# A first head pair's attention output recombined in chunks of 128, spread over the second pair's attention

## The chip, the cores and the metric

The kernel runs on one core of a Trainium2 chip. The metric is the device time of one execution in microseconds (us); lower is better. Three executions of the kernel before gave 1064.78, 1065.20 and 1062.72 us, with a median of 1064.78 us. On-chip data lies in 128 partitions, and five engines work side by side, each through its own queue in strict order: TensorE (PE: matmuls, and transposes done as matmuls), VectorE (DVE), ScalarE (ACT), GpSimd (POOL), and SyncE (SP), whose queue issues every DMA of this kernel. An instruction that waits holds up everything behind it in its engine's queue.

## The reference

One layer of a hybrid decoder: four token mixers share an input projection, each result is gated by SiLU, and an output projection, a norm and the residual follow. The part that matters here is mixer A, attention with four heads of 64 channels over 2048 positions:

```python
def _dilated_mixture(q, k, v):
    outs, lses = [], []
    for window, dil in ((128, 1), (512, 4), (2048, 16)):
        o, lse = _dilated_branch(q, k, v, window, dil, slopes)
        outs.append(o); lses.append(lse)
    w = jax.nn.softmax(jnp.stack(lses), axis=0)
    return jnp.einsum('gbhs,gbhsd->bhsd', w, jnp.stack(outs))
...
y = jnp.concatenate([ya * silu(ag), yb * silu(bg), yc * silu(cg), yd * silu(dg)], -1)
y = jnp.einsum('bse,ed->bsd', y, w_out)
return x + _rms_norm(y, post_g)
```

Every head thus has three branch outputs (dilation 4, 16 and 1, in the kernel's order), which are weighted per position by three factors, added, and multiplied by the gate.

## The kernel before

**Stages.** The first stage (to about 684 us in the profile) makes all projections and mixers B, C and D. The second runs attention for two pairs of heads, and fills TensorE's free time with the part of the output projection that needs only mixers B, C and D (`partial`, for nine of the sixteen token tiles, results to memory `part_d`). The third (`final`) finishes the output projection, the norm and the residual.

**Attention.** `attention(p)` handles the heads 2p and 2p+1, one after the other. For each head it loads q and k (`q2`, `k2a`, `k2b`) and, for each of three branches, the values (`att_v`); the tiles rotate through a ring of seven. `branch` computes scores on TensorE (`ps_s`), adds the bias and takes the row minimum on VectorE (`att_p`, line 639), exponentiates on ScalarE (line 641), transposes on TensorE (`ps_pt`), splits into a high and a low part on ScalarE and VectorE (`pt_hi` line 648, `pt_lo` line 649), multiplies with the values (`ps_o`), and adds two halves of the result into the output `att_o` (ScalarE line 663, VectorE line 664). The tile `att_p` has `B_PR` = 6 buffers. A pair has three output tiles of 128 x 2048 numbers: two in one tile `o01`, and `o2` for dilation 1. `o01` of the first pair lies in the pool `big`, that of the second in the pool `po`; `o2` of both pairs lies in `po`, under one tag with one buffer.

**Weights of the branches.** After the third branch of a head, `weigh` computes the three factors and writes them to memory (`f_d`, shown as `fd`).

**Combine.** `combine` goes over the positions in chunks. For a chunk it loads the factors of both heads, each broadcast over 64 partitions (`fb`, lines 763), and the gate (`sga`, line 765); multiplies and adds on GpSimd (lines 766, 767) and VectorE (768, 769, 770, 772); splits the result on ScalarE and GpSimd (`ysa`, lines 776, 777), and stores it (`ya`, line 779). For the first pair the chunk is 256 positions (eight chunks), `fb`, `sga` and `ysa` have two buffers each, so the load of chunk i+2 needs chunk i's buffers.

**Order.** A scheduler orders each engine's queue by its own estimate of durations, with earlier written code preferred; `tc.issue_after(mark)` holds a block back until the scheduler has placed the marked instruction. `marks` lists the attention's value matmuls; the `partial` calls are spread over them. The first pair's `combine` is written ahead of the second pair's attention.

Of the kernel before, what the change touches and what calls it, by code (L numbers as in the profile page):

```python
# [9 lines left out]
F32 = mybir.dt.float32  # L10
# [8 lines left out]
P = 128  # L19
SEQ = 2048  # L20
# [16 lines left out]
MASKED = 1e30  # L37
PB = {"part": 1, "fin": 8}
N_S, N_T, N_O = 2, 3, 2
CORD = (2, 3, 0, 1)  # L40
CB0, B_PR, B_PT = 2, 6, 3


def mix_constants():
# [41 lines left out]
def hymba(ctx: ExitStack, tc: tile.TileContext, x, pre_g, w_in, sgu_g, sgu_w, sgu_b, pool_w,  # L86
# [4 lines left out]
    def r32(ap):  # L91
        return ap.bitcast(F32)
# [450 lines left out]
    def out_weights(i, eng):  # L543

        w = big.tile([P, 2, 2, DM], F32R, tag="big", name=f"wo{i}")
        for e in range(2):
            raw = p3.tile([P, DM], F32, tag="z", bufs=2, name="wo_raw")
            D.dma_start(raw, wo_src[:, i * 2 + e])
            A.activation(w[:, e, 0], raw, AF.Copy)
            eng.tensor_tensor(w[:, e, 1], raw, r32(w[:, e, 0]), ALU.subtract)  # L550
            wo[i * 2 + e] = (w[:, e, 0], w[:, e, 1])

    marks = []

    def attention(p, tab):
        o01 = (big if p == 0 else po).tile([P, 2, SEQ], F32, tag="big" if p == 0 else "o01", name="att_o01")
        o = [o01[:, 0], o01[:, 1], po.tile([P, SEQ], F32, tag="o2", name="att_o2")]
        for s in range(2):
            h = 2 * p + s
            rows = slice(s * HD, (s + 1) * HD)  # L560
# [191 lines left out]
        V.tensor_tensor(ew, ew, nm.unsqueeze(1).broadcast_to([P, 3, 16]), ALU.mult)  # L752
        D.dma_start(f_d[h].rearrange("b (q f) -> q b f", f=16), ew)

    def combine(p, o, pool, bufs, keep, step, order):

        kept = {}
        nb = step // P
        for c0 in order:
            cs = slice(c0, c0 + step)  # L760
            fb = pool.tile([P, 3, step], F32, tag="fb", bufs=bufs, name="fb")
            for s in range(2):
                D.dma_start(fb[s * HD:(s + 1) * HD], f_d[2 * p + s][:, cs].partition_broadcast(HD))
            sg = pool.tile([P, step], F32, tag="sga", bufs=bufs, name="sga")
            D.dma_start(sg, ag_d[p][:, cs])
            G.tensor_tensor(fb[:, 1], fb[:, 1], o[1][:, cs], ALU.mult)
            G.tensor_tensor(fb[:, 2], fb[:, 2], o[2][:, cs], ALU.mult)
            V.tensor_tensor(fb[:, 0], fb[:, 0], o[0][:, cs], ALU.mult)
            V.tensor_tensor(fb[:, 0], fb[:, 0], fb[:, 1], ALU.add)
            V.tensor_tensor(fb[:, 0], fb[:, 0], fb[:, 2], ALU.add)  # L770
            y = fb[:, 1]
            V.tensor_tensor(y.rearrange("p (n i r) -> p n r i", n=nb, r=16),
                            fb[:, 0].rearrange("p (n r i) -> p n r i", n=nb, r=16),
                            sg.rearrange("p (n r i) -> p n r i", n=nb, r=16), ALU.mult)
            ys = pool.tile([P, 2, step], F32R, tag="ysa", bufs=4 if keep else CB0, name="ysa")
            A.activation(ys[:, 0], y, AF.Copy)
            (V if keep else G).tensor_tensor(ys[:, 1], y, r32(ys[:, 0]), ALU.subtract)
            if not keep:
                D.dma_start(ya_d[c0 // GRP][:, :, c0 % GRP:c0 % GRP + step], r32(ys))
            kept[c0 // step] = ys  # L780
        return kept

    def load_y(t, pool):
# [29 lines left out]
    def partial(t):  # L813
        z = p3.tile([P, DM], F32, tag="z", bufs=2, name="z")
        ys = split_y(load_y(t, p3), p3, G)
        for n in range(2):
            A.activation(z[:, n * GRP:(n + 1) * GRP], out_proj(ys, range(2, 8), n, ps2, "part"), AF.Copy)
        D.dma_start(part_d[t * P:(t + 1) * P], z)
# [34 lines left out]
    po = ctx.enter_context(tc.tile_pool(name="po", bufs=1, side="right", reuse_waits="tile"))  # L853
    with ExitStack() as c2:
        pm = c2.enter_context(tc.tile_pool(name="pm", bufs=1, reuse_waits="tile"))
        p2 = c2.enter_context(tc.tile_pool(name="p2", bufs=1, reuse_waits="tile"))
        ps2 = c2.enter_context(tc.tile_pool(name="ps2", bufs=2, space=PSUM, reuse_waits="tile"))
        tab = pm.tile([P, T_HEAD], F32, name="tab")
        D.dma_start(tab, catt)
        o = attention(0, tab)  # L860
        for i in (1, 2, 3):
            out_weights(i, V if i == 2 else G)
        combine(0, o, p2, 2, False, 256, range(0, SEQ, 256))
        o = attention(1, tab)
        for t in range(npart):
            with tc.issue_after(marks[int(len(marks) * (t + spread[0]) / npart * spread[1])]):
                partial(t)
        out_weights(0, G)
# [5 lines left out]
    post_b = p4.tile([P, DM], F32, name="post_b")  # L874
    ya = [[p4.tile([P, 2, GRP], F32R, tag="ya0", bufs=4, name="ya0") for g in range(NG)]]
    ya.append(combine(1, o, p4, 2, True, GRP, [c * GRP for c in CORD]))
    for g in CORD:
        D.dma_start(r32(ya[0][g]), ya_d[g])
    D.dma_start(post_b, post_g[0].partition_broadcast(P))
    order = full[:3]  # L880
# [33 lines left out]
```

## Time and profile before

| | before |
|---|---|
| median of three executions | 1064.78 us |
| the profiled execution's own time | 1066.84 us |
| its span, first to last instruction | 1065.1 us |
| TensorE matmuls busy | 993.5 us (93%) |
| VectorE busy | 540.4 us (51%) |
| ScalarE busy | 379.6 us (36%) |
| GpSimd busy | 190.9 us (18%) |
| mean granted TensorE clock | 0.973 |
| bytes moved by DMA | 135.27 MB |

Times in the profile count from the first instruction. "Idle before, releaser" says how long an engine had been idle before an instruction and what it then waited for. A table by stretches gives, for each stretch of time, the busy microseconds of each engine, the clock that TensorE was granted (1.00 is full speed) and the share of time for which the 16 DMA engines were busy. SPq rows are DMA issues; the time in such a row is that of the issue, not of the transfer.

### The profile page before, as it was taken

The numbers are of one execution on the slowest core, as the hardware profiler recorded it, in microseconds if no ns is written. First come the engines' busy times: TensorE is split into PE (matmuls) and PEld (weight loads), VectorE is DVE, ScalarE is ACT, GpSimd is POOL, SyncE is SP. The second block draws the span as 40 slices with busy tenths as digits, with TensorE's granted clock in tenths as the row PEclk, the third lists the DMA queues.
The fourth block names the chain that finished last, engine by engine and source line by source line (L and its number), as shares of the span: only waits on it lengthen the run. The fifth ranks groups of instructions, "written<-read, shape, count | busy, mean of one in ns | idle before, by whom it ended". The sixth has DMA issues, their size and how long they took to land. (4 is left out here: it accounts for less than half of the span.)

```text
span 1065.1 us, 15690 instructions
## 1 busy us (share of the span) xinstructions
PE 993.5 (93%) x5916; PEld 855.0 (80%) x5916; DVE 540.4 (51%) x1547; ACT 379.6 (36%) x851; POOL 190.9 (18%) x195
## 2 busy tenths in 40 slices
PE   5899999999999999999999999979998779988993
PEld 5888898988877988989898787778988569867872
DVE  7611216696332422023763321287776677547898
ACT  6320222131222421122211121498877448513231
POOL 2310012211232000002210134031122351142000
PEclk9999999999999999999999999998999879989997
DMA  8530313233223331042211830395659953484776
GB/s 279 147 99 20 100 60 114 85 120 92 86 79 99 99 100 39 25 135 80 80 41 50 210 119 20 116 213 162 147 168 201 207 152 85 109 270 129 268 259 217
DMA packets 119962, 135.27 MB, mean 127 GB/s; under 512 B 14928, under 2 KB 95952, under 8 KB 117840
## 3 DMA queue, kind: packets, MB, share of 16 engines
q1 hardware_dynamic: 119888, 134.29, 43.6%
q8 instruction: 46, 0.75, 0.3%
q14 instruction: 28, 0.23, 0.1%
HBM read 97.80 MB, written 36.47 MB: 126 GB/s over the span
## 5 line engine op out<-in xcount | busy, mean ns | idle before, releaser
L95 PE MATMUL ps_t<-hh,w 128*128 128x512 f32 x1152 | 370.1, 398 | 2.3 <-DVE b_t L370 2.3
L95 PEld LDWEIGHTS ps_t<-hh,w 128*128 128x128 f32 x1152 | 216.7, 189 | 52.4 <-issue 3.4
L95 PE MATMUL ps_t<-hl,w 128*128 128x512 f32 x576 | 227.6, 395 | 0.0
L95 PE MATMUL ps_m<-w,hh 128*128 128x256 f32 x1024 | 183.8, 282 | 2.0 <-ACT hh L230 1.6
L95 PE MATMUL ps_out<-wo,yt 128*128 128x512 f32 x576 | 155.6, 414 | 6.1 <-DVE yt L798 3.1
L95 PEld LDWEIGHTS ps_m<-w,hh 128*128 128x128 f32 x1024 | 157.5, 190 | 3.9 <-ACT hh L230 2.8
L95 PE MATMUL ps_m<-w,hl 128*128 128x256 f32 x512 | 145.4, 284 | 0.2 <-DVE hl L231 0.2
L95 PEld LDWEIGHTS ps_out<-wo,yt 128*128 128x128 f32 x576 | 109.8, 198 | 31.1 <-DVE yt L798 4.4
L95 PEld LDWEIGHTS ps_t<-hl,w 128*128 128x128 f32 x576 | 108.7, 189 | 24.3 <-issue 1.4
L250 DVE TENSOR_TENSOR w<-raw,w 128x1024 fp32r<-128x1024 f32 x42 | 59.0, 1412 | 109.6 <-ACT w L248 109.4
L95 PEld LDWEIGHTS ps_m<-w,hl 128*128 128x128 f32 x512 | 97.6, 191 | 0.8 <-DVE hl L231 0.4
L641 ACT ACTIVATE att_p<-att_p,att_st 128x128 f32<-128x128 f32 (+1 forms) x192 | 86.4, 453 | 20.5 <-DVE att_st L639 20.0
L248 ACT ACTIVATE w<-raw 128x1024 fp32r<-128x1024 f32 (+1 forms) x56 | 55.0, 997 | 70.1 <-PE ps_t L95 37.6
L639 DVE CUSTOM_DVE_ANT_0 att_p<-ps_s,tab 128x128 f32<-128x128 f32 (+1 forms) x192 | 60.3, 357 | 34.5 <-PE ps_s L95 31.0
L95 PE MATMUL ps_o<-pt_hi,att_v 128*128 128x128 f32 (+1 forms) x204 | 54.4, 287 | 6.2 <-DVE att_o L664 4.2
L649 DVE TENSOR_TENSOR pt_lo<-ps_pt,pt_hi 128x512 fp32r<-128x512 f32 x80 | 51.2, 650 | 12.5 <-ACT pt_hi L648 12.1
L95 PE MATMUL ps_o<-pt_lo,att_v 128*128 128x128 f32 (+1 forms) x204 | 52.8, 294 | 3.5 <-DVE pt_lo L649 3.4
L98 PE MATMUL ps_pt<-ident,att_p 128*128 128x128 f32 x300 | 51.2, 283 | 0.8 <-ACT att_p L641 0.8
L95 PEld LDWEIGHTS ps_o<-pt_hi,att_v 128*128 128x128 f32 x204 | 40.8, 200 | 9.5 <-DVE att_o L664 4.6
L648 ACT ACTIVATE pt_hi<-ps_pt 128x512 fp32r<-128x512 f32 x80 | 44.1, 563 | 11.2 <-PE ps_pt L98 5.7
L95 PE MATMUL ps_s<-k2a,q2b 128*128 128x128 f32 (+1 forms) x128 | 37.5, 325 | 8.6 <-DMA k2a<-qk 4.4
L95 PEld LDWEIGHTS ps_o<-pt_lo,att_v 128*128 128x128 f32 x204 | 40.6, 199 | 5.9 <-DVE pt_lo L649 4.8
(160 smaller groups left out, 1319.8 us busy)
## 6 DMA issues: line engine op xcount, KB each, us to landing
raw<-in_w_in_dram SPq DMA_DIRECT2D x52, 512.0 KB
qk<-qk_s SPq DMA_DIRECT2D x16, 512.0 KB
att_v<-vd SPq DMA_DIRECT2D x8, 1024.0 KB
xr<-in_x_dram SPq DMA_DIRECT2D x16, 512.0 KB
out_dram<-z SPq DMA_DIRECT2D x15, 512.0 KB
xt<-in_x_dram SPq DMA_DIRECT2D x7, 1024.0 KB
yraw<-yb SPq DMA_DIRECT2D x16, 384.0 KB
partd<-z SPq DMA_DIRECT2D x9, 512.0 KB
```

Of the source, the lines that this page charges most:

```text
L95: return T.matmul(o, lhsT, rhs, start=start, stop=stop, skip_group_check=True)
L98: T.transpose(o, i, ident[:n, :n])
L248: A.activation(hi, raw[:, :, cs], AF.Copy, scale=sc)
L250: eng.tensor_tensor(lo, raw[:, :, cs], r32(hi), ALU.subtract)
L639: V.tensor_tensor_reduce(out=pr[:, u, :w], in0=ps[:, u, :w], in1=bb, scale=-SLOPES[h] * HD ** -0.5, scalar=3e38, op0=ALU.add, op1=ALU.min, ...
L641: A.activation(pr[:, u, :w], pr[:, u, :w], AF.Exp, bias=neg, scale=-1.0, accum_out=st[:, 1, n:n + 1])
L648: A.activation(hi, pt[:, :w], AF.Copy)
L649: V.tensor_tensor(lo, pt[:, :w], r32(hi), ALU.subtract)
```

## The change

Four edits belong together. The first pair's `o2` moves from the pool `po` into the pool `p2`, so that the two pairs no longer share memory for it. `B_PR` goes from 6 to 5, and the chunk from 256 to 128 positions, which frees the memory for it. `combine` is divided into a load and a piece of work per chunk; for the first pair the load of chunk i+1 is written ahead of the work of chunk i, and both are held back to a mark: sixteen marks spread evenly over the first 75% of the second pair's value matmuls (`PACE`). The call moves behind the second pair's attention. The second pair's own `combine` computes as before. All line numbers behind the constants shift by one, those of `combine` by up to seven, those behind it by sixteen and more.

```diff
+PACE = 0.75
-CB0, B_PR, B_PT = 2, 6, 3
+CB0, B_PR, B_PT = 2, 5, 3
...
-        o = [o01[:, 0], o01[:, 1], po.tile([P, SEQ], F32, tag="o2", name="att_o2")]
+        o = [o01[:, 0], o01[:, 1], (po if p else p2).tile([P, SEQ], F32, tag="o2", name="att_o2")]
...
-    def combine(p, o, pool, bufs, keep, step, order):
+    def combine(p, o, pool, bufs, keep, step, order, after=None):
         kept = {}
         nb = step // P
-        for c0 in order:
+        todo = list(order)
+        def load(c0):
             cs = slice(c0, c0 + step)
             fb = pool.tile([P, 3, step], F32, tag="fb", bufs=bufs, name="fb")
             for s in range(2):
                 D.dma_start(fb[s * HD:(s + 1) * HD], f_d[2 * p + s][:, cs].partition_broadcast(HD))
             sg = pool.tile([P, step], F32, tag="sga", bufs=bufs, name="sga")
             D.dma_start(sg, ag_d[p][:, cs])
+            return fb, sg
+
+        def work(c0, fb, sg):
+            cs = slice(c0, c0 + step)
             G.tensor_tensor(fb[:, 1], fb[:, 1], o[1][:, cs], ALU.mult)
...
             kept[c0 // step] = ys
+
+        if after is None:
+            for c0 in todo:
+                work(c0, *load(c0))
+            return kept
+        ahead = load(todo[0])
+        for i, c0 in enumerate(todo):
+            with after(i):
+                now, ahead = ahead, load(todo[i + 1]) if i + 1 < len(todo) else None
+                work(c0, *now)
         return kept
...
-        combine(0, o, p2, 2, False, 256, range(0, SEQ, 256))
+        o0, n0 = o, len(marks)
         o = attention(1, tab)
+        pace = (len(marks) - n0) * PACE / (SEQ // P)
+        combine(0, o0, p2, 2, False, P, range(0, SEQ, P), lambda i: tc.issue_after(marks[int(n0 + (i + 0.5) * pace)]))
```

On SP's queue, where every load is issued, the place is the beginning of the second head of the second pair: its keys (`k2b`) stand among the combine's transfers. `sga` is a gate load, `fb` a load of one head's factors, `ya` a store of a finished chunk, `std` and `partd` are other stores. Before:

```order
L765 DMA sga<-agd_71 128x256 x2
L779 DMA ya_73<-ysa 256x1x256
L763 DMA fb<-fd_86 64x3x256
L779 DMA ya_73<-ysa 256x1x256
L763 DMA fb<-fd_87 64x3x256
L763 DMA fb<-fd_86 64x3x256
L763 DMA fb<-fd_87 64x3x256
L735 DMA std_84<-sT 16x16x8 x2
L818 DMA partd<-z 128x1024
L569 DMA k2b<-qk_69 64x2048 x2
```

Now:

```order
L785 DMA ya_73<-ysa 256x1x128
L765 DMA fb<-fd_86 64x3x128
L765 DMA fb<-fd_87 64x3x128
L785 DMA ya_73<-ysa 256x1x128
L765 DMA fb<-fd_86 64x3x128
L765 DMA fb<-fd_87 64x3x128
L736 DMA std_84<-sT 16x16x8 x2
L767 DMA sga<-agd_71 128x128
L570 DMA k2b<-qk_69 64x2048 x2
L767 DMA sga<-agd_71 128x128
```

The transfers are half as wide, and the gate load of the fifth chunk, which needs the third chunk's buffer, now stands ahead of the keys. In both orders the factors of a chunk follow the store of the chunk two before it.

On VectorE the place is between the third and the fifth chunk before (the first row is the third chunk's last product, the last row the fifth chunk's first):

```order
L772 TENSOR_TENSOR fb<-fb,sga 128x2x16x8
L649 TENSOR_TENSOR pt_lo<-ps_pt,pt_hi 128x512
L770 TENSOR_TENSOR fb<-fb 128x256
...
L772 TENSOR_TENSOR fb<-fb,sga 128x2x16x8
L649 TENSOR_TENSOR pt_lo<-ps_pt,pt_hi 128x512 x2
L639 ISA att_p,att_st<-ps_s,tab 128x256
L639 ISA att_st 128x1
L639 ISA att_p,att_st<-ps_s,tab 128x256
L639 ISA att_st 128x1
L768 TENSOR_TENSOR fb<-fb,att_o_5880 128x256
```

and now between the thirteenth and the fifteenth chunk, where the first and the last row have the same meaning:

```order
L778 TENSOR_TENSOR fb<-fb,sga 128x16x8
L774 TENSOR_TENSOR fb<-fb,att_o_5880 128x128
...
L775 TENSOR_TENSOR fb<-fb 128x128
L665 TENSOR_TENSOR att_o_7131<-ps_o,att_o_7131 64x4x16x8
L640 ISA att_p,att_st<-ps_s,tab 128x256
L640 ISA att_st 128x1
L640 ISA att_p,att_st<-ps_s,tab 128x256
L640 ISA att_st 128x1
L776 TENSOR_TENSOR fb<-fb 128x128
L778 TENSOR_TENSOR fb<-fb,sga 128x16x8
L650 TENSOR_TENSOR pt_lo<-ps_pt,pt_hi 128x512
L774 TENSOR_TENSOR fb<-fb,att_o_5880 128x128
```

The dots stand for two `att_p` rows of 256 in each list, in the second with one `pt_lo` row of 512. A chunk's products are now mixed with attention rows up to the end of the second pair, where they stood together in its first half before.

## The prediction

> **What bounds the kernel now.** I read the head of the page first, then a table by stretches of the attention and final stages.
>
> ```profile
> PE 993.5 (93%) x5916; PEld 855.0 (80%) x5916; DVE 540.4 (51%) x1547; ACT 379.6 (36%) x851; POOL 190.9 (18%) x195
> ```
>
> TensorE is busy for 93% of the span, so time is won only where it idles or runs at a low clock.
>
> ```profile
> core 0: us, PE busy (x) PEld busy (x) DVE busy (x) ACT busy (x) POOL busy (x), PEclk, DMA share, GB/s
> 684.00:800.00 116.00, 105.32 (x737) 96.11 (x738) 87.72 (x327) 100.44 (x308) 22.94 (x22) 0.96 0.69 178
> 800.00:880.00 80.00, 64.71 (x354) 54.67 (x353) 54.04 (x166) 42.24 (x136) 30.83 (x37) 0.85 0.81 187
> 880.00:920.00 40.00, 40.00 (x289) 37.21 (x289) 29.24 (x99) 33.26 (x101) 4.56 (x6) 0.99 0.25 59
> 920.00:960.00 40.00, 33.82 (x136) 26.17 (x136) 17.49 (x23) 8.05 (x15) 12.91 (x8) 0.91 0.79 242
> ```
>
> The stretch 800 to 880 us is the one with the combine of the first pair. TensorE idles 80.00 - 64.71 = 15.3 us there, and its clock is 0.85; of the 64.71 busy us, 0.15 x 64.71 = 9.7 us are due to the clock. Right behind, with the combine over, it idles not at all. So 25.0 us is what the stretch can give. What it waits for is in the list of waits of that stretch:
>
> ```profile
> DVE fb L768 <- DMA fb<-fd: 17.6, 5, 5.0
> ...
> ACT att_o L663 <- POOL fb L767: 5.9, 1, 5.9
> ...
> PE ps_st L98 <- DVE pt_lo L649: 3.7, 1, 3.7
> PE ps_s L95 <- DVE att_st L639: 3.4, 2, 3.2
> PE ps_o L95 <- DVE att_o L664: 3.3, 3, 2.4
> PE ps_o L95 <- DVE pt_lo L649: 2.9, 2, 2.7
> ```
>
> TensorE waits for VectorE's attention rows, and VectorE has been standing before a combine row whose factors had not landed: five times, 17.6 us. The second row is the shared memory: ScalarE's first write into the second pair's `o2` waits 5.9 us for GpSimd's last read of the first pair's. In order of time:
>
> ```profile
> 869.78 0.90 POOL L767 TENSOR_TENSOR fb<-fb,att_o 128x256 f32<-128x256 f32 x1
> ...
> 870.72 1.08 ACT L663 ACTIVATE att_o<-ps_o 64x512 f32<-64x512 f32 x2 [5.87 <-POOL fb L767]
> ...
> 872.85 0.33 PE L95 MATMUL ps_o<-pt_hi,att_v 128*128 128x128 f32 x1 [2.38 <-DVE att_o L664]
> ...
> 875.12 0.44 PE L95 MATMUL ps_o<-pt_hi,att_v 128*128 128x128 f32 x1 [0.54 <-DVE att_o L664]
> ```
>
> Thus 2.4 + 0.5 us of TensorE's idle time are due to `o2`; with the clock after it (0.84 on 16.50 busy us, 2.6 us) this is 5.5 us:
>
> ```profile
> 800.00:820.00 20.00, 17.27 (x116) 15.63 (x114) 13.32 (x56) 13.33 (x51) 5.80 (x8) 0.91 0.89 183
> ...
> 860.00:880.00 20.00, 16.50 (x75) 13.47 (x74) 13.58 (x31) 7.36 (x20) 8.60 (x10) 0.84 0.59 136
> ```
>
> The other 19.5 us belong to the 17.6 us of waits for factors: 1.1 us lost for each us VectorE waits.
>
> **The change part by part.** *Memory of its own for `o2`.* It takes away 5.5 us, whole: the reads of the first pair's `o2` then hold up nothing.
>
> *The first wait stays.* The first chunk needs the second head's factors, which exist only when that head's weights are stored.
>
> ```profile
> 804.96 1.26 SPq L763 DMA_DIRECT2D fb<-fd  x2
> ...
> 810.00 0.42 DVE L768 TENSOR_TENSOR fb<-fb,att_o 128x256 f32<-128x256 f32 x1 [4.85 <-DMA fb<-fd]
> ...
> 811.08 0.39 PE L95 MATMUL ps_o<-pt_lo,att_v 128*128 128x256 f32 x1 [2.73 <-DVE pt_lo L649]
> ...
> L639 DVE CUSTOM_DVE_ANT_0 att_p<-ps_s,tab 128x128 f32<-128x128 f32 x38 | 9.0, 281 | 1.7 <-PE ps_s L95 1.7
> ```
>
> The two loads are issued at 804.96, and VectorE stands until 810.00. In the new order the first two chunks' rows stand four narrow `att_p` rows earlier (4 x 0.281 = 1.1 us, the last row). I keep the 2.7 us gap, the clock (0.09 x 17.27 = 1.6 us) and add that with a small copy, 1.3 us: 5.6 us. Bounds: 3 (half the bytes land sooner) to 7.
>
> *The waits behind it* decide. A chunk's load follows the store of the chunk two before, in both orders. So VectorE's wait is the turnaround (last product, split, store issued, factors issued, landed) less the attention work that stands between. Before:
>
> ```profile
> 835.53 0.59 DVE L772 TENSOR_TENSOR fb<-fb,sga 128x256 f32<-128x256 f32 x1
> ...
> 837.58 0.60 DVE L772 TENSOR_TENSOR fb<-fb,sga 128x256 f32<-128x256 f32 x1
> ...
> 840.23 0.55 SPq L779 DMA_DIRECT2D ya<-ysa  x1
> 840.83 1.28 SPq L763 DMA_DIRECT2D fb<-fd  x2
> ...
> 846.21 0.43 DVE L768 TENSOR_TENSOR fb<-fb,att_o 128x256 f32<-128x256 f32 x1 [4.97 <-DMA fb<-fd]
> ...
> 850.95 0.43 DVE L768 TENSOR_TENSOR fb<-fb,att_o 128x256 f32<-128x256 f32 x1 [1.12 <-DMA fb<-fd]
> ```
>
> The fourth chunk's product ends at 838.18, the sixth's factors have landed at 850.95: 12.8 us. The third's ends at 836.12, the fifth starts at 846.21: 10.1 us, of which VectorE worked 5.1 and stood 4.97. For the work between I use the mean rows:
>
> ```profile
> L649 DVE TENSOR_TENSOR pt_lo<-ps_pt,pt_hi 128x512 fp32r<-128x512 f32 x28 | 18.9, 683 | 5.4 <-ACT pt_hi L648 5.3
> L639 DVE CUSTOM_DVE_ANT_0 att_p<-ps_s,tab 128x256 f32<-128x256 f32 x42 | 16.2, 415 | 6.2 <-PE ps_s L95 4.1 <-PE ps_pt L98 2.0
> L664 DVE TENSOR_TENSOR att_o<-ps_o,att_o 64x512 f32<-64x512 f32 x21 | 14.4, 685 | 1.9 <-ACT att_o L663 1.5
> ```
>
> In the new order, from the thirteenth chunk's product to the fifteenth's first row, stand four `att_p` (1.66), two `pt_lo` (1.37), one `att_o` (0.69) and about 1.5 us of combine rows: 5.2 us. VectorE is 29.24/40 = 73% busy in an undisturbed stretch, so 5.2 us take 7.1 us to pass. Done so for all fourteen chunks from the third on, the work between is 8.4, 8.6, 5.9, 9.0, 9.5, 4.4, 5.4, 5.7, 7.0, 7.8, 7.8, 5.8, 4.8 and 6.2 us (rough sums), or 11.5, 11.8, 8.1, 12.3, 13.0, 6.0, 7.4, 7.8, 9.6, 10.7, 10.7, 7.9, 6.6 and 8.5 us of time. A turnaround of 8 us leaves waits of 4.3 us in all, 10 us leaves 18 us, 11 us leaves 27 us. I take 8: all of the head's large loads, which share the DMA engines (share 0.81), are gone after the first third (share 0.25 from 880 on), the first load, unhindered on SP, landed 3.8 us after its second issue ended (806.22 to 810.00), and the steps ahead of it were 2.05 us (838.18 to 840.23) plus 1.8 us of issues: 7.7 us. Loss: 4.3 x 1.1 = 4.7 us.
>
> *Smaller pieces.* The per-chunk cost need not halve:
>
> ```profile
> L768 DVE TENSOR_TENSOR fb<-fb,att_o 128x256 f32<-128x256 f32 x8 | 4.2, 530 | 17.6 <-DMA fb<-fd 17.6
> ...
> L768 DVE TENSOR_TENSOR fb<-fb,att_o 128x512 f32<-128x512 f32 x4 | 3.9, 965 | 16.5 <-DMA fb<-fd 16.5
> ...
> L770 DVE TENSOR_TENSOR fb<-fb 128x256 f32<-128x256 f32 x8 | 6.0, 756 | 0.0
> ...
> L770 DVE TENSOR_TENSOR fb<-fb 128x512 f32<-128x512 f32 x4 | 4.9, 1235 | 0.0
> ```
>
> A line through 256 and 512 columns leaves 2 x 530 - 965 = 95 ns and 2 x 756 - 1235 = 277 ns at zero width; the other two rows lie in that band. Four rows for eight more chunks are 8 x 4 x 0.1 to 0.28 = 3 to 9 us of VectorE, spread over some 105 us in which it is idle for a quarter of the time; I charge 1 us (0 to 4). SP issues 32 more transfers (16 factors at 1.28/2 = 0.64 us, 8 stores and 8 gates at no more than the 0.55 of a store: 19 us), hidden as long as SP is not what a load waits for; if it is, the turnaround above grows.
>
> *One `att_p` buffer less* also reorders the first pair. In 684 to 800 us ScalarE is busy for 100.44 of 116 us behind those same tiles, so a fifth instead of a sixth in flight should not starve TensorE: 0, between -2 and +4 us.
>
> *The tail.* The second pair's last factors now stand ahead of the reload of the first pair's result, the last output weights behind the factors of its last chunk.
>
> ```profile
> 937.86 0.33 SPq L548 DMA_DIRECT2D wo_raw<-in_w_out_dram  x1
> ...
> 948.17 0.69 DVE L768 TENSOR_TENSOR fb<-fb,att_o 128x512 f32<-128x512 f32 x1 [12.05 <-DMA fb<-fd]
> ```
>
> Both happen while TensorE has the final tiles' other matmuls. Of the 6.2 us it idles from 920 to 960, the earlier factors could return all, and late weights could double it: 0, between -6 and +6.
>
> Sum: 25.0 - 5.6 - 4.7 - 1 = 13.7 us. The profiled execution took 1066.84 us (span 1065.1), so it would come to 1053.1; the median is 1064.78, 2.06 lower, and comes to **1051 us**.
>
> **The rivals.** *The waits only move (1066 us).* A turnaround of 10 us: 18 x 1.1 = 20 us of loss, 25.0 - 5.6 - 20 - 1 = -1.6. For it speaks that a load's time hardly follows its size. In the chain of waits:
>
> ```profile
> 861.35 7.16 DMA fb<-fd
> ...
> 965.09 9.73 DMA fb<-fd
> ```
>
> The first is 192 KB, the second 384 KB: twice the bytes, a third more time. Against it: both ran among large loads. The Trainium skill, page "DMA: Bandwidth & Descriptors", section "Anatomy of one DMA — SWDGE (gpsimd) path", gives a DMA about 2.0 us fixed plus its bytes at 436 GB/s, for the other issue path; an estimate by it saves 0.2 us when 192 KB become 96, so by that page a smaller chunk alone buys no shorter turnaround, as the two rows here suggest too.
>
> *Head of line on VectorE (1076 us, slower).* A turnaround of 11 us, because SP is late: it holds loads behind waits for other engines and has 32 issues more. Then 27 x 1.1 = 30 us are lost at fourteen places, each short of attention work behind it, against 19.5 us at five before: 25.0 - 5.6 - 30 - 1 = -11.6. It decides from a turnaround of 10.2 us, and the 12.8 us seen once speak for it. The keys `k2b` of the last head would be late too: they now follow a gate load that needs the third chunk done.
>
> *All of it is won (1041 us).* No waits but the first one's shortest: 25.0 - 3 + 2 from the reorder. TensorE's work would then leave no idle time at all, with VectorE at (54.04 + 29.24 + 3)/96 = 90%, where the stretches above have it at 76% and less.
>
> **How the numbers follow.** A measurement of this kernel tells about 0.3% (3.2 us) from no change. Forecast 0.58, all won 0.08 (both faster); waits only move 0.15 (same); head of line 0.19 (slower). So faster 0.66, same 0.15, slower 0.19. The forecast alone, with turnarounds of 7 to 9 us and the other bounds, spans 1044 to 1060; the range of 8 in 10 reaches down to 1041, the ceiling, and up to 1070, into the slower case.
>
> **What would show it.** Right: no wait of ScalarE's line 664 (663 before) for GpSimd; VectorE's waits for `fb` in the second pair's attention under 12 us in all, the first of them the longest; the clock at 0.95 or more from 820 us to the end of the attention, which ends 10 to 15 us earlier. Wrong: waits for `fb` of 2 us or more at most chunks, with the gaps on SP ahead of their issue (then the turnaround failed); TensorE waiting for `k2b`; a longer first pair (the `att_p` buffer); or the attention earlier and the tail longer by as much.

## The result, and the profile after

| | before | after |
|---|---|---|
| median of four executions | 1064.94 us (1062.72 to 1065.20) | 1087.68 us (1085.94 to 1090.31) |
| ratio, 95% interval | | 1.0224 [1.0201, 1.0247] |
| span of the profiled execution | 1065.1 us | 1088.6 us |

The change makes the kernel 2.2% slower. 1051 us were predicted, so both the sign and the size were wrong, and the range (1041 to 1070) does not hold it. Of the rivals, "head of line on VectorE" (1076 us) came nearest: VectorE stands at the head of its queue at most chunks, for longer than was priced. The reason that the rival gives, a late SP, is only a small part of it, as is shown below.

The head of the page of the kernel after, engines by busy time:

```profile
PE 1005.4 (92%) x5916; PEld 865.2 (79%) x5916; DVE 536.9 (49%) x1579; ACT 380.7 (35%) x859; POOL 192.4 (18%) x219
```

VectorE has 32 instructions more than before and 3.5 us less of busy time: more work on VectorE is not what costs. Where the 22.7 us went is seen when the second pair's attention is cut at the points where a head's factors are stored. The issues of those stores (`fd`) stand at 799.10, 876.87 and 928.73 us before and at 797.85, 876.79 and 946.33 us after. The two rows of each kernel are the pair's first and second head; columns as in the tables above (length; busy us of PE, PEld, DVE, ACT, POOL; granted clock; DMA share; GB/s). Before:

```profile
799.10:876.87 77.77, 62.48 (x350) 53.02 (x349) 52.69 (x165) 41.95 (x137) 29.95 (x37) 0.87 0.82 187
876.87:928.73 51.86, 50.59 (x333) 45.51 (x333) 35.76 (x117) 38.16 (x110) 6.95 (x9) 0.97 0.35 89
```

After:

```profile
797.85:876.79 78.94, 66.90 (x373) 58.03 (x373) 48.05 (x180) 45.30 (x145) 21.60 (x38) 0.84 0.63 155
876.79:946.33 69.54, 54.84 (x298) 45.17 (x298) 38.77 (x134) 35.03 (x108) 18.89 (x34) 0.92 0.41 96
```

The first head is no shorter, although only nine of the sixteen chunks begin in it now. The second head was undisturbed before (1.3 us idle) and now takes 17.7 us more: it got the other seven chunks. What is behind 946.33 us also grew, from 136.4 to 142.3 us. TensorE's idle time in the attention went from 16.6 to 26.7 us, and the clock took 15.1 us of its busy time (0.16 x 66.90 + 0.08 x 54.84) instead of 9.6. These two make 15.6 of the 18.9 us by which the attention is longer; the other 3.2 us are more matmul work at full speed that lies in it (106.7 us for 103.4).

The waits that end in the attention of the second pair of the kernel after (engine, line, what it waited for; us in total, times, longest us):

```profile
POOL fb L772 <- DMA fb<-fd: 66.2, 14, 7.8
DVE fb L774 <- DMA fb<-fd: 50.0, 15, 5.7
ACT att_p L642 <- DVE att_st L640: 45.2, 17, 7.8
```

VectorE stands before a chunk's factors fifteen times instead of five, and for 50.0 us instead of 17.6. The row of ScalarE waiting for GpSimd's last read of `o2` is gone, as it should be. The third row is one way on: ScalarE waits for the attention rows that stand behind the factors in VectorE's queue. TensorE mostly waits for such rows directly; its two largest waits in this stretch are

```profile
PE ps_s L96 <- DVE att_st L640: 6.8, 3, 2.5
PE ps_o L96 <- DVE pt_lo L650: 5.8, 5, 2.4
```

and its waits for ScalarE's `att_p` come to 2.6 us.

One round of a factor tile in order of time. Only the rows of this tile's two chunks and the first products of the chunk between are shown; the attention's rows between them are left out:

```profile
867.93 0.37 DVE L778 TENSOR_TENSOR fb<-fb,sga 128x128 f32<-128x128 f32 x1
868.38 0.31 ACT L782 ACTIVATE ysa<-fb 128x128 fp32r<-128x128 f32 x1
872.73 0.29 DVE L774 TENSOR_TENSOR fb<-fb,att_o 128x128 f32<-128x128 f32 x1 [4.43 <-DMA fb<-fd]
872.76 0.57 POOL L772 TENSOR_TENSOR fb<-fb,att_o 128x128 f32<-128x128 f32 x1 [7.15 <-DMA fb<-fd]
873.29 0.45 POOL L773 TENSOR_TENSOR fb<-fb,att_o 128x128 f32<-128x128 f32 x1
873.71 0.45 POOL L783 TENSOR_TENSOR ysa<-fb,ysa 128x128 fp32r<-128x128 f32 x1
...
874.18 0.55 SPq L785 DMA_DIRECT2D ya<-ysa  x1
874.79 1.27 SPq L765 DMA_DIRECT2D fb<-fd  x2
...
882.33 0.29 DVE L774 TENSOR_TENSOR fb<-fb,att_o 128x128 f32<-128x128 f32 x1 [3.94 <-DMA fb<-fd]
```

A chunk's last product ends at 868.30, and ScalarE's copy at 868.69. The split on GpSimd (line 783), the last reader of the factor tile, runs only at 873.71: on GpSimd it stands behind the *next* chunk's products (line 772), which wait 7.15 us for *their* factors. Then come the store (0.55 us), the two issues (to 876.06), and the landing at 882.33, 6.3 us behind the last issue, with a DMA share of 0.42 in this time. The turnaround is 882.33 - 868.30 = 14.0 us. So in this round the two tiles do not overlap as two should: one chunk's reload is issued only when the other's has landed. Four loads of values (`att_v`, 256 KB each) are issued from 877.26 on, while the factors are on their way. Over the fourteen turnarounds of this kernel, measured in the same way, the mean is 12.8 us. VectorE worked in 6.2 us of it and stood 5.8 us for factors: 3.2 us for those at the end of the turnaround, the rest for those of the chunk between. The three parts of the turnaround, as means over the fourteen, beside what the prediction assumed:

| part | assumed, us | measured, us |
|---|---|---|
| product's end to the store's issue | 2.05 | 4.3 |
| store's issue to the end of the factors' last issue | 1.8 | 2.2 |
| from there to VectorE's next product (the landing) | 3.8 | 6.3 |
| turnaround | 7.7, taken as 8 | 12.8 |

The split is not always late: it starts 0.5 to 7.7 us behind the product.

### The profile page after: what moved, and what is told of

Read it like the earlier page. It is cut to its first block, busy times and chain, and to the rows that moved or that the text cites. A ratio compares the mean times of both kernels' runs of the same rounds, so it can differ in the third digit from the quotient of the medians.

```text
span 1088.6 us, 15868 instructions
## 1 busy us (share of the span) xinstructions
PE 1005.4 (92%) x5916; PEld 865.2 (79%) x5916; DVE 536.9 (49%) x1579; ACT 380.7 (35%) x859; POOL 192.4 (18%) x219
## 4 chain that ended last, share of the span: by engine, by line
PE 68%; DMA 16%; DVE 8%; issue 2%; SPq 2%; ACT 2%; POOL 1%; DVEq 0%; POOLq 0%; ACTq 0%
PE ps_t L96 37%; PE ps_m L96 15%; DMA fb<-fd 6%; PE ps_out L96 5%; PE ps_s L96 2%; DMA out_dram<-z 2%; PE ps_o L96 2%; PE ps_of L96 2%; PE ps_pt L99 2%; DMA z<-partd 1%; DMA k2b<-qk 1%; DMA cm<-in_cmix_dram 1%; DVE z L866 1%; PE ps_in L96 1%; DMA raw<-in_w_in_dram 1%
## 5 line engine op out<-in xcount | busy, mean ns | idle before, releaser
L96 PEld LDWEIGHTS ps_t<-hh,w 128*128 128x128 f32 x1152 | 215.9, 188 | 49.2 <-issue 3.3
L96 PE MATMUL ps_out<-wo,yt 128*128 128x512 f32 x576 | 159.8, 417 | 14.9 <-DVE yt L814 9.4
L99 PE MATMUL ps_pt<-ident,att_p 128*128 128x128 f32 x300 | 57.8, 300 | 8.9 <-DVE sT L725 5.5
L96 PE MATMUL ps_o<-pt_hi,att_v 128*128 128x128 f32 (+1 forms) x204 | 58.6, 303 | 4.6 <-DVE att_o L665 3.6
L96 PE MATMUL ps_o<-pt_lo,att_v 128*128 128x128 f32 (+1 forms) x204 | 56.9, 311 | 6.4 <-DVE pt_lo L650 6.1
L650 DVE TENSOR_TENSOR pt_lo<-ps_pt,pt_hi 128x512 fp32r<-128x512 f32 x80 | 51.2, 649 | 6.2 <-ACT pt_hi L649 5.8
L96 PEld LDWEIGHTS ps_o<-pt_lo,att_v 128*128 128x128 f32 x204 | 43.1, 211 | 10.3 <-DVE pt_lo L650 9.1
L96 PEld LDWEIGHTS ps_o<-pt_hi,att_v 128*128 128x128 f32 x204 | 43.5, 213 | 8.6 <-DVE att_o L665 2.4
L649 ACT ACTIVATE pt_hi<-ps_pt 128x512 fp32r<-128x512 f32 x80 | 44.7, 563 | 9.8 <-PE ps_pt L99 8.0
L99 PEld LDWEIGHTS ps_pt<-ident,att_p 128*128 128x128 f32 x300 | 37.8, 151 | 12.7 <-ACT att_p L642 4.9
```

The lines of the kernel that those rows point to most:

```text
L96: return T.matmul(o, lhsT, rhs, start=start, stop=stop, skip_group_check=True)
L99: T.transpose(o, i, ident[:n, :n])
L649: A.activation(hi, pt[:, :w], AF.Copy)
L650: V.tensor_tensor(lo, pt[:, :w], r32(hi), ALU.subtract)
```

## The experiments

All times are medians; the ratio is to the kernel before, measured beside each group of runs on the same chip (1061.5 to 1063.9 us). "Waits" are VectorE's waits for `fb` in the second pair's attention.

**Is it the spreading, the chunk or the memory?** First the changed kernel with the combine ahead of the attention again, everything else kept:

```diff
-        o0, n0 = o, len(marks)
+        combine(0, o, p2, 2, False, P, range(0, SEQ, P))
         o = attention(1, tab)
-        combine(0, o0, p2, 2, False, P, range(0, SEQ, P), lambda i: tc.issue_after(marks[int(n0 + (i + 0.5) * pace)]))
```

> The changed kernel without the spreading: o2 in memory of its own, chunks of 128, five att_p buffers, but the combine written ahead of the second pair's attention as before, each chunk's load with its work. Theory one (VectorE stands before factors that have not landed, because sixteen chunks with two buffers have a turnaround of some 13 us and are placed by a schedule that takes it for shorter): the waits stay about as many, since the chunks and the buffers stay; VectorE waits 40 to 55 us for factors in the second pair's attention and the time is 1080 to 1092 us. Theory two (the spreading is at fault: it carries the combine into the second half of the attention, where before there was none): the waits come back to the kernel before's 18 to 25 us and the time to 1060 to 1068 us.

Measured: 1088.83 us, 1.0255 [1.0207, 1.0302], waits 48.8 us at 13 places. Spreading neither costs nor saves anything that can be told.

Then the kernel before with chunks of 128 and nothing else (`range(0, SEQ, P)` and `P` in place of 256):

> The kernel before with chunks of 128 in place of 256 and nothing else: o2 shared, six att_p buffers, combine ahead of the second pair's attention. What the runs so far show: VectorE stands some 3 to 4 us before nearly every chunk's factors wherever the combine lies, five times before, thirteen to fifteen times with sixteen chunks. Theory one (each chunk's load, not the place of the combine nor the memory, is what costs; the order puts the first product where the load was thought to land, and it lands some 4 us later): sixteen chunks alone give 40 to 55 us of waits and, with the second pair's o2 waiting for the sixteenth chunk too, 1080 to 1095 us. Rival (the loads are only late when the attention is interleaved with them to its end): below 1072 us.

Measured: 1089.90 us, 1.0285 [1.0235, 1.0336]. The rows of VectorE for factors and of ScalarE for `o2`, in the attention of the second pair of this kernel:

```profile
DVE fb L768 <- DMA fb<-fd: 45.7, 13, 7.0
...
ACT att_o L663 <- POOL fb L767: 1.8, 1, 1.8
```

The smaller chunk alone brings the whole loss. At this chunk size the memory for `o2` makes no difference beyond the intervals (1.0285 without, 1.0255 with it).

These two kernels also show that the late split is not needed for the loss. Their stores are issued 2.1 and 1.8 us behind the product in the mean, near the 2.05 us that the prediction assumed, and their mean turnarounds are 11.8 and 10.6 us. They still wait 48.8 and 45.7 us, because VectorE finds less work between (5.9 and 3.7 us for 6.2) and the landing is as long as in the changed kernel or longer (7.1 and 6.7 us).

The buffer count alone, the kernel before with `B_PR` = 5:

> The kernel before with five att_p buffers instead of six. My step: between -2 and +4 us, so 1063 to 1069 us. Rival (the buffer is what costs): 1075 us or more.

Measured: 1063.97 us, 1.0013 [0.9989, 1.0037]. It costs nothing, as predicted.

**How much could be won?** The changed kernel without the first pair's factor loads:

```diff
-            for s in range(2):
+            for s in range(2 if keep else 0):
...
+            f = [fb[:, j] if keep else o[j][:, cs] for j in range(3)]
-            G.tensor_tensor(fb[:, 1], fb[:, 1], o[1][:, cs], ALU.mult)
+            G.tensor_tensor(fb[:, 1], f[1], o[1][:, cs], ALU.mult)
```

and so for the other two. The first pair's outputs are multiplied by themselves, so its weighting by the factors is left out, and every product keeps its size and engine.

> The changed kernel, but the first pair's combine does not load its factors: the three outputs are multiplied with themselves instead, so this part of the result is left out; every other load, product and store is kept. Theory one: without these loads VectorE stands nowhere in the second pair's attention, TensorE fills up, and the attention from the last factor store of the first pair to that of the second shrinks from 148.5 us to 105 to 115 us; the time is 1040 to 1055 us. Rival (the sixteen chunks' products and SP's transfers themselves are too much, spread through the attention): the time stays above 1075 us.

Measured: 1038.63 us, 0.9786 [0.9744, 0.9829]. The stretch of 800 to 880 us in this kernel:

```profile
800.00:880.00 80.00, 78.37 (x528) 69.91 (x527) 65.12 (x254) 64.46 (x208) 25.30 (x48) 1.00 0.62 161
```

TensorE idles 1.6 us instead of 15.3, at full clock, with the first products of ten of the sixteen chunks in this stretch; the other six run from 763 us on, since nothing waits for the factors now. The time is a little better than either theory had it. The ceiling that I had put at 25.0 us is there, and the products do not stand in its way. The run takes away the loads and the wait for the weights together, so it does not price the transfers apart from the waits. Against the changed kernel the difference of the ratios is 0.0438, or 47 us (49 us by the medians), for 50.0 us of waits: about 1 us lost for each us that VectorE stands.

**The split out of GpSimd's queue.** The split of line 783 moves to VectorE (`V.tensor_tensor(ys[:, 1], ...)`).

> The changed kernel with the low part of the split (the last step ahead of a chunk's store) on VectorE instead of GpSimd for the first pair too. In the changed kernel the store of a chunk is issued 1.0 to 9.4 us, in the mean 4.4 us, after its product, partly because GpSimd's split of one chunk stands behind GpSimd's multiplications of the next chunk, which wait for that chunk's factors. Theory A (this coupling of two chunks on GpSimd is a main part of the turnaround): product to store falls to about 2 us, the turnaround from 13 to about 10 us, VectorE's waits from 50 to 25 us, the time to 1065 to 1075 us. Theory B (SP's order and the landing make the turnaround): the waits stay at 45 us or more and the time at 1083 to 1092 us.

Measured: 1081.91 us, 1.0195 [1.0141, 1.0249]; waits 43.5 us at 15 places, mean turnaround 11.8 us, and 3.1 us from product to store instead of 4.3. This lies between the two theories, nearer to B, and its interval overlaps that of the changed kernel. On VectorE the split can stand behind the next chunk's first product as well, so this removes only a part of the delay.

**Spread further.** The marks over the whole attention (`PACE = 1.0`).

> The changed kernel with the sixteen chunks spread over all of the second pair's value matmuls in place of 75%. Undisturbed, the attention of the pair took 99.9 us without the loads, so two chunks are 9.4 us apart at 75% and 12.5 us at 100%; the measured turnaround is 13 us. Theory one, first form (a wait is the turnaround less the work placed between): the waits fall from 50 us to 15 to 30 us, the attention by 10 to 20 us; the last chunks come late for the final stage, which gives a few us back: 1068 to 1080 us. Second form (every load is misjudged by the same 4 us, since the order always puts the product where the load was thought to land): the waits stay above 40 us, 1083 to 1093 us.

Measured: 1086.70 us, 1.0243 [1.0203, 1.0282]; waits 51.2 us at 15 places. In this kernel the rows of every engine, and SP's issues, come in the same order as in the kernel after; VectorE's busy time between a chunk's product and the product two chunks later is the same to within 0.02 us at all fourteen places. So the places of the marks, over three quarters or over all of the attention, did not decide the order, neither here nor in the change, and the run is in effect a second measurement of the kernel after. What a wider spread would do is not shown. That the coming round of the tiles sets the order instead is likely, but argued.

**More tiles.** Three factor tiles instead of two (`combine(0, o0, p2, 3, ...)`, `B_PR` = 4 for the memory).

> The changed kernel with three buffers for factors and gate instead of two, paid for with four att_p buffers instead of five. A chunk's load is then released by the chunk three before it: at 75% these are 14 us apart, above the measured turnaround of 13 us. Theory one, first form: the waits fall from 50 us to under 20 us and the time to 1045 to 1065 us. Second form (the order puts the products earlier as soon as buffers are free): the waits stay above 35 us, 1075 us or more. If the fourth att_p buffer is what costs, the time rises with the waits gone.

Measured: 1075.71 us, 1.0134 [1.0103, 1.0165]; waits 32.7 us at 11 places. Some 40% of the loss is gone (1.3% instead of 2.2%), but it stays slower than before.

**An earlier release.** The last product goes into the tile that is stored, in place, so that the factor tile is free at VectorE's product and not at GpSimd's split:

```diff
-            y = fb[:, 1]
+            ys = pool.tile([P, 2, step], F32R, tag="ysa", bufs=4 if keep else CB0, name="ysa")
+            y = fb[:, 1] if keep else r32(ys[:, 1])
...
-            ys = pool.tile([P, 2, step], F32R, tag="ysa", bufs=4 if keep else CB0, name="ysa")
```

In the changed kernel:

> The changed kernel, but the last product of a first-pair chunk is written to the tile that is stored (ysa) and not back into the factors' tile. The factors' tile is then free at VectorE's last product, not after GpSimd's split. The late-release theory: in the changed kernel a factor load is issued only after GpSimd's split of the chunk two before, and that split stands on GpSimd behind the next chunk's products, which themselves wait for that chunk's factors, so two buffers work almost as one and the turnaround is 13 us. With the release at the product the turnaround is about 9 us, the waits of VectorE for factors in the second pair's attention are 10 to 18 us instead of 50, and the time is 1050 to 1058 us. The landing theory: the order of the instructions takes a load for some 4 us shorter than it is, so that VectorE meets every load some 3.5 us early whenever it was issued: 13 to 15 waits, 45 to 50 us, and 1083 to 1088 us.

Measured: 1078.60 us, 1.0139 [1.0095, 1.0184]. The row of waits, and one round, in this kernel (the second fence leaves out the rows of other engines):

```profile
DVE fb L774 <- DMA fb<-fd: 40.2, 14, 7.6
```

```profile
859.83 0.37 DVE L779 TENSOR_TENSOR ysa<-fb,sga 128x128 f32<-128x128 f32 x1
860.27 1.24 SPq L765 DMA_DIRECT2D fb<-fd  x2
...
862.72 0.55 SPq L785 DMA_DIRECT2D ya<-ysa  x1
...
866.81 0.29 DVE L774 TENSOR_TENSOR fb<-fb,att_o 128x128 f32<-128x128 f32 x1 [2.24 <-DMA fb<-fd]
```

The profiled execution was the fastest of the four (1072.77 us). The release works in this round: the load is issued 0.07 us behind the product, ahead of the store, and the turnaround is 6.6 us. But over all fourteen the mean falls only from 12.8 to 10.7 us. From the product to the first issue it is 1.9 us in the mean instead of 5.0, since in some rounds SP is held by other transfers; the landing stays at 6.6 us; and the work that VectorE has between falls too, from 6.2 to 5.4 us. That was in neither expectation: the late-release theory had 10 to 18 us of waits, the landing theory 45 to 50, and 40.2 were measured. A likely reason for the lesser work is that the scheduler places the next product by its own estimate of the landing: when a tile comes free earlier it places the product earlier too. No run shows its estimate.

The same edit in the kernel before:

> The kernel before (chunks of 256, shared o2, ahead of the attention) with only that edit: the last product into ysa. Late-release theory: the fourth and fifth waits and the sixth's get shorter by the 2 to 4 us between the product and the split's end; of 17.6 us of waits 8 to 11 remain, 1055 to 1060 us. Landing theory: the same five waits of 3.5 us and 1064 us.

Measured: **1051.19 us, 0.9884 [0.9849, 0.9919]**. This is faster than both kernels. Its two heads, cut as above, and its waits up to the end of the attention:

```profile
796.05:867.41 71.36, 59.30 (x350) 51.39 (x348) 49.68 (x165) 41.75 (x136) 29.85 (x37) 0.93 0.88 210
867.41:917.43 50.02, 49.33 (x339) 44.90 (x340) 35.52 (x117) 38.32 (x112) 6.07 (x8) 1.00 0.33 87
```

```profile
DVE fb L768 <- DMA fb<-fd: 19.2, 7, 4.4
...
ACT att_o L663 <- POOL fb L767: 2.3, 1, 2.3
```

The time is better than the late-release theory expected, but not for its reason: VectorE's waits did not fall (19.2 us for 17.6). The turnaround fell from 12.0 to 9.0 us, the combine ends 66.2 us behind the factors' store instead of 76.4, the wait on the shared `o2` falls from 5.9 to 2.3 us, and the clock in the first head rises from 0.87 to 0.93. The attention is 8.2 us shorter; another 4.1 us lie behind it and 3.1 ahead of it, and what brought those is open.

**Loads two chunks ahead.** Product into `ysa`, three factor tiles, `B_PR` = 4, and at each mark the load of chunk i+2:

```diff
-        ahead = load(todo[0])
+        ahead = [load(c0) for c0 in todo[:bufs - 1]]
         for i, c0 in enumerate(todo):
             with after(i):
-                now, ahead = ahead, load(todo[i + 1]) if i + 1 < len(todo) else None
-                work(c0, *now)
+                if i + bufs - 1 < len(todo):
+                    ahead.append(load(todo[i + bufs - 1]))
+                work(c0, *ahead.pop(0))
```

> As the run before it (product into ysa), with three factor tiles and loads two chunks ahead instead of one, and four att_p buffers. Late-release theory: a load has a whole chunk more to land, no wait but the first and the time is 1043 to 1050 us, near the 1039 us of the kernel without the factor loads. Landing theory: the rows are now held by the marks of the spreading and not by the landing, so most waits go as well, if the marks come later than the landing; where the order runs ahead of the marks the waits stay: 20 to 30 us of waits, 1060 to 1070 us.

Measured: 1071.17 us, 1.0076 [1.0047, 1.0104]; waits 22.7 us at 11 places, and a new one: VectorE now writes `ysa` and waits 8.8 us, three times, for the stores of its two buffers. The 1043 to 1050 us of the late-release theory are missed by far; the 20 to 30 us of waits of the landing theory hold, and its 1060 to 1070 us nearly.

**Rounds or loads?** By now the waits seemed to go by how often the tiles come round. Two runs with product into `ysa` were to tell it apart: sixteen chunks of 128 over four tiles (`B_PR` = 3), which come round as often as eight chunks over two, and eight chunks of 256 over three tiles (`B_PR` = 4).

> The changed kernel with the last product into ysa and four factor tiles of 128 columns (three att_p buffers). The sixteen chunks then come round four times, as in the kernel before with its eight chunks of 256 and two tiles. Rounds theory: 4 rounds of 5 us, 20 us of waits, 1055 to 1062 us. Rival, a price of each load: 11 to 15 waits of 2 to 3 us, 1070 to 1078 us.

> The kernel before with the last product into ysa and three factor tiles instead of two (four att_p buffers pay for the third). Rounds theory: what is lost goes by how often all factor tiles come round, some 5 us of waits a round, and not by the number of chunks or of bytes; eight chunks over three tiles are 2.7 rounds instead of 4, so the waits for factors in the second pair's attention fall from 19 to about 13 us and the time from 1051 to about 1045 us. Rival, a price of each load: eight loads as before, seven waits of 2.7 us, 1051 us.

Measured: four tiles of 128, 1067.15 us, 1.0039 [1.0024, 1.0054]; three of 256, 1051.99 us, 0.9893 [0.9870, 0.9917]. VectorE's rows, of the former:

```profile
DVE fb L774 <- DMA fb<-fd: 23.2, 10, 5.7
```

and of the latter, up to the end of the attention:

```profile
DVE fb L768 <- DMA fb<-fd: 10.5, 6, 4.0
```

By the rounds 20 and 13 us of waits were expected. The latter run speaks for them: by the load it would have been 19 us. The former does not tell: 23.2 us are also the lower end of what the rival has, 11 to 15 waits of 2 to 3 us. The times do not follow the rounds all the way: 1067 instead of 1055 to 1062, and 1052 instead of 1045, which is the time that the price of each load gives. Both pay for the tiles with `att_p` buffers, and three of 256 have VectorE waiting for stores of `ysa` too (6.1 us); how much of the time this explains was not measured.

**Memory of its own, by itself.** At 256 it has room only with `B_PR` = 4 and `B_PT` = 2, so a control has the same buffers and the shared memory.

> The kernel before (chunks of 256 ahead of the attention), with memory of its own for the first pair's third tile; four att_p buffers and two of pt_hi and pt_lo pay for it. Against the next run, which has the same buffers and the shared memory, this gives the term of 5.5 us of the prediction by itself. The prediction: 5.5 us less than the next run. Rival: the wait on GpSimd's last read is one of several that end together, and VectorE's wait for the last factors stands in its place: 0 to 2 us.

> The kernel before with four att_p buffers and two of pt_hi and pt_lo, and nothing else: the control of the run before it. If the buffers cost nothing, 1064 us; if the attention lives from them, 1070 us or more.

Measured: with its own memory 1067.29 us, 1.0034 [1.0014, 1.0053]; the control 1079.64 us, 1.0151 [1.0129, 1.0172]. TensorE's waits for the attention's additions, with its own memory:

```profile
PE ps_o L95 <- DVE att_o L664: 5.9, 2, 4.3
```

and in the control:

```profile
PE ps_o L95 <- DVE att_o L664: 15.1, 4, 7.2
```

Memory of its own wins 12.4 us between these two, more than the 5.5 us of the prediction and far more than the 0 to 2 us of the rival. But the wait that made up the 5.5 us is not in the control as such: ScalarE stands 4.8 us for VectorE at a chunk's split (to 882.73 in that profile), right ahead of its first two additions into `o2`; GpSimd's last read of the first pair's `o2` ends at 882.13. TensorE's longest wait, 7.2 us, ends behind these additions. The rest of the 12.4 us is not taken apart. The buffers cost 1.5% (the control), more than the memory brings back.

All runs that keep the factor loads, by rounds (chunks over tiles):

| kernel | rounds | waits, us (times) | us a round | time, us |
|---|---|---|---|---|
| after | 8 | 50.0 (15) | 6.3 | 1087.7 |
| full pace (order as after) | 8 | 51.2 (15) | 6.4 | 1086.7 |
| own memory, not spread | 8 | 48.8 (13) | 6.1 | 1088.8 |
| before, 128 | 8 | 45.7 (13) | 5.7 | 1089.9 |
| split on VectorE | 8 | 43.5 (15) | 5.4 | 1081.9 |
| after, into `ysa` | 8 | 40.2 (14) | 5.0 | 1078.6 |
| three tiles | 5.3 | 32.7 (11) | 6.1 | 1075.7 |
| two ahead, into `ysa` | 5.3 | 22.7 (11) | 4.3 | 1071.2 |
| four tiles, into `ysa` | 4 | 23.2 (10) | 5.8 | 1067.2 |
| before, `B_PR` 5 | 4 | 21.2 (5) | 5.3 | 1064.0 |
| before | 4 | 17.6 (5) | 4.4 | 1064.9 |
| before, into `ysa` | 4 | 19.2 (7) | 4.8 | 1051.2 |
| control, 256 | 4 | 16.5 (7) | 4.1 | 1079.6 |
| own memory, 256 | 4 | 15.0 (6) | 3.8 | 1067.3 |
| before, three, into `ysa` | 2.7 | 10.5 (6) | 3.9 | 1052.0 |

A round costs 3.8 to 6.4 us of VectorE's waits, with half as many bytes in it at 128 as at 256 for the same tiles. By the load, the same waits are 1.3 (three of 256) to 3.2 us (full pace), so rounds describe them better. It is a description, with a spread of its own: from three tiles (two ahead) to four, both into `ysa`, the waits do not fall. Among kernels of about the same waits (15 to 23 us) the times still lie between 1051 and 1080 us: the wait on `o2` and the attention's buffers are prices of their own.

## Why the prediction was wrong

**What bounds the kernel: right.** The 25.0 us to be won in 800 to 880 us were there: without the loads the ratio is 0.9786, which is 22.8 us of 1064.94 (18.2 to 27.3 by the interval). The forecast of the rival "all of it is won", 1041 us, was this ceiling. The price of 1.1 us for each us of wait held nearly (about 1).

**Memory of its own: right in kind.** The wait that was to go is gone after the change. What it is worth differs by the kernel: 12.4 us between the runs at 256 with fewer buffers, where the wait that the prediction read does not appear as such, and nothing that can be told at 128, where the wait on `o2` was 1.8 us and not 5.9 to begin with.

**The first wait: right in size.** It is 4.41 + 0.89 us in the kernel after; 4.85 us before. What it cost TensorE was not taken apart.

**The waits behind it: the step that failed.** "A turnaround of 8 us leaves waits of 4.3 us in all ... I take 8." The turnaround was 12.8 us. By the prediction's own list of work between the chunks this gives 47.5 us of waits (the sum of what each of the fourteen elapsed times lacks of 12.8), and 50.0 - 4.41 - 0.89 = 44.7 us were measured. So the mis-sized term is enough for the sign; the prediction's sum with 44.7 us in place of 4.3 gives 25.0 - 5.6 - 49.2 - 1 = -30.8 us, 8 us more loss than was measured.

By the table above the 8 us were short at two places. They assumed 3.8 us from the last issue to the landing; it took 6.3 us. They assumed that the split follows the product at once; the store was issued 4.3 us behind it, in part because GpSimd stood before the next chunk's factors. SP's own part grew by 0.4 us only. The 3.8 us were misread, too: the two issues at 804.96 belong to two chunks (the first head's factors of both were issued at 750.70), and the load that VectorE waited for is the earlier one, whose issue ended at about 805.6; it took 4.4 us.

The trace of before had six turnarounds, 10.1 to 12.8 us, 12.0 in the mean, and the prediction quoted two of them. It argued them away by the crowded DMA engines. The crowd is a part: in the kernel after the landing took 7.7 us in the mean in the four rounds with a DMA share of 0.79 or more, and 5.9 us in the nine later ones that VectorE waited for, with shares of 0.26 to 0.68. But 5.9 us without the crowd are still 2.1 us above the 3.8.

**A second fault lies in the formula's use.** It treats the work between two chunks as given, so the near agreement of 47.5 and 44.7 us is partly luck: the listed times have a mean of 9.4 us, made of 6.9 us of work and idle time as in an undisturbed stretch, and the trace has 9.6 us, made of 6.2 us of work, 2.6 us of waits for the chunk between and 0.8 us of other idle time. By the same list the 10.6 us of the kernel before with chunks of 128 would give 23 us of waits, and it has 45.7 (the list is that of another order). The runs with an early release show the same: the turnaround fell by 2.1 us and the work between by 0.8 (12.0 to 9.0 and 6.1 to 4.7 in the kernel before), as if the order were made with a shorter landing than the chip's. A better turnaround thus does not come back whole. That the waits go by rounds would fit: each time the tiles come round, the program meets the loads too early again. This link is argued; a scheduler with another estimate of the landing was not tried, and why VectorE finds so little work between stays open. Halving the chunk with the same two tiles doubled the rounds from 4 to 8, and the waits went from 17.6 to 45.7 us. The prediction counted in turnaround and work and never counted rounds.

**Smaller pieces (1 us) and `B_PR` (0): right**, by VectorE's busy time and the run with five buffers. **The tail (0, within 6 us): inside its bounds, at the edge.** It grew by 5.9 us. TensorE's longest idle time behind the attention, in the kernel after:

```profile
957.53 0.69 DVE L774 TENSOR_TENSOR fb<-fb,att_o 128x512 f32<-128x512 f32 x1 [11.24 <-DMA fb<-fd]
...
964.38 4.21 PE L96 MATMUL ps_out<-wo,yt 128*128 128x512 f32 x9 [9.41 <-DVE yt L814]
```

The splits of `yt`, which the first final tiles need, stand in VectorE's queue behind the second pair's first products, which wait for their own factors for 11.2 us. Before, these products waited as long (12.05 us), but TensorE's waits for `yt` came to 3.1 us only. In the 46 us behind the attention TensorE is busy for 36.1 us after and 41.2 us before, which is most of the 5.9 us; why the order there differs was not tried.

**The rivals.** "Waits only move" and "head of line" are the same mechanism at 10 and 11 us of turnaround. The latter's words, "It decides from a turnaround of 10.2 us, and the 12.8 us seen once speak for it", were right; a chance of 0.19 was too small when five of the six turnarounds before lay above 10.2 us and the sixth at 10.1. Its reason was not: SP's issues brought 0.4 of the 4.8 us by which the turnaround was longer than 8, and TensorE did not wait for `k2b`. The prediction's own sign of being wrong came: waits for `fb` of 2 us or more at eleven of the sixteen chunks.

## What to carry to other kernels

Count how often the buffers of a late load come round: while an in-order engine meets each round some microseconds before it lands, halving the pieces with the same number of buffers doubles the rounds, and here the waits grew by more than that. Look for the last reader of the buffer and at what stands ahead of it on its engine; here it could be a split behind the next chunk's own wait, and writing the product to another tile made the kernel before 1.2% faster, though only a part of that is explained. Check that a control such as the marks changes the order at all before its effect is discussed. When a trace has measurements of the quantity on which everything rests, take all of them rather than a sum of best cases.

## What the runs showed of the hardware

A load of two times 96 KB, broadcast to 64 partitions each, landed 6.3 us behind its last issue in the round quoted (DMA share 0.42 in those 6.3 us); one of two times 192 KB in the kernel before took 6.7 us (issues to 839.49, used at 846.21 after a wait; DMA share 0.96). With the DMA engines about as busy (share about 0.8 and more), the smaller loads took 7.7 us in the mean of four and the larger 7.1 us in the mean of the four that VectorE waited for. Half the bytes saved nothing that can be seen. The Trainium skill, page "DMA: Bandwidth & Descriptors", section "Anatomy of one DMA — SWDGE (gpsimd) path", gives about 2.0 us fixed plus the bytes at 436 GB/s for the other issue path, an estimate of 2.2 us for 96 KB: the runs agree that the size hardly matters and show about three times the fixed part for these broadcasts from SP.

The clock was lower where TensorE's work came in pieces: 0.84 in the first head after (12.0 us idle of 78.94), 1.00 in 800 to 880 us without the factor loads (1.6 us idle). So a wait can cost twice, once as idle time and once in the matmuls behind it; in the attention after, 26.7 us of idle time stand beside 15.1 us of lower clock. The two do not go in proportion: the second head after idles more (14.7 us of 69.54) at a higher clock (0.92).
